# Pooled maps and row tails of a hybrid encoder step, set later behind their projections, and the first half's maps moved to another pair of PSUM banks

## The chip, the cores and the metric

The kernel runs on one core of one Trainium2 chip. The metric is the device time of one execution in microseconds (us), as the median of several runs. A core has five engines that work at the same time, each through its own list of instructions and strictly in the order of that list: TensorE (PE in the profile; PEld is its weight load), VectorE (DVE), ScalarE (ACT), GpSimd (POOL) and SyncE (SP), whose list holds DMA issues. An instruction that waits for another engine's result holds up everything behind it in its own list.

## The reference, cut to what matters

One layer over a prompt of 2048 frames and 64 frames of a second stream. The part that the change touches is the B-branch: `u`, one of the blocks of the input projection, is averaged over a trailing window, mapped by a small matrix per group, scaled and gated.

```python
z = h @ w_in                                  # q, k, v, ga, u, gb, mg, side by side
...
for g, w in enumerate(POOL_WINDOWS):          # 2, 4, 8, 16; 256 channels each
    outs.append((hi - lo) / cnt - uf[..., sl])            # trailing mean minus self
p = jnp.einsum('btgc,gcd->btgd', p.reshape(b, t, 4, 256), w_pool)      # the map
pb = p.reshape(b, t, POOL_WIDTH) * pool_scale
...
y_b = (pb * jax.nn.silu(gb)) @ w_br_b         # the gate rows: silu(gb)
...
pp_l.append(u[:, -POOL_BUF:])                 # last 15 rows of u go out: the tails
```

## The kernel before

All matrices are float32. A product is done in three matmuls, with each operand split into a high and a low part (`hi` and `lo`; the casts and subtractions of line 82 and 83 make the parts).

The rows are worked in two halves: half 0 holds 1024 prompt frames and the 64 frames of the second stream, half 1 the other 1024 prompt frames. Channels stand on the partitions, frames along the free dimension. `proj` does one slab of 128 output channels: per row group (512, 256 and 320 frames wide in half 0; twice 512 in half 1) it runs 24 matmuls into one PSUM tile named `pj` (lines 319 to 321), then calls an evacuation, and it hands control back after every six matmuls, so also in the middle of a row group. PSUM is given out in pools of two tiles for each of the names `pj`, `z`, `tr` and `att`, eight banks in all.

`pool_group` does one window group: two slabs of `u`. Their evacuation (`evac_u`) copies the rows to SBUF (line 395), saves the last 15 columns in `hist` (line 396) and, for the 64 frames, in `shist` (line 403), sums over the window on DVE (lines 368 and 377, in `pooled`), and splits the result into `phi` and `plo`, of which three buffers each exist. Behind the second slab come two maps (`mapped`), one for each 128 output channels: six matmuls (lines 423 to 425) into one PSUM tile, then one DVE instruction that scales by `pscale` and multiplies by the gate row `gbl` (line 427), and a store. `tail_out` turns the 15 saved rows on PE (line 437), copies them on ACT (line 439) and stores them.

Beside half 0's later projections runs the attention of the 64 frames (`sample_stream`): key chunks turned into `tr` tiles (line 761), scores into two `z` tiles (lines 780 and 781), which ACT copies (line 785) and DVE adds up (line 786), then sigmoids, a scan (line 622) and products (line 830). Half 1's pooled groups stand alone between projections.

What order stands on PE is set by a planner in the kernel. It keeps a clock of estimated matmul time in ns; `run` takes from several generators in turn; `defer(delay, fn)` puts a piece of work aside until that clock has gone on by the delay, and `settle`, called after every step of `run`, does what is due. PE's list is then kept as written. The lists of DVE, ACT, POOL and SP are ordered, in these stages, by the framework's scheduler from the same program.

Of the kernel before, what the change touches and what calls it, by code (L numbers as in the profile page):

```python
# [8 lines left out]
F32 = mybir.dt.float32  # L9
# [6 lines left out]
P = 128  # L16
# [7 lines left out]
RA = SEQ // 2 + DEC  # L24
# [20 lines left out]
def kernel(  # L45
# [6 lines left out]
    nc = tc.nc  # L52
# [12 lines left out]
    gb_d = dram.tile([D, R], F32, name="gb_d")  # L65
# [11 lines left out]
    def split(hi, lo, src, eng=None):  # L77

        if eng == "v":
            nc.vector.tensor_copy(hi, src)  # L80
        else:
            nc.scalar.copy(hi, src)  # L82
        (nc.gpsimd if eng == "g" else nc.vector).tensor_tensor(lo, src, hi.bitcast(F32), op=ALU.subtract)  # L83
# [23 lines left out]
    def mm_ns(n):  # L107
        return max(107.0, n * 0.4167)

    def defer(delay, fn):  # L110
        waiting.append((clock[0] + delay, fn))
# [37 lines left out]
    with ExitStack() as front:  # L149
        pool = front.enter_context(tc.tile_pool(name="front", bufs=1, side="left"))  # L150
        psum = front.enter_context(tc.tile_pool(name="fpsum", bufs=2, space=PSUM))
# [3 lines left out]
        attp = attx.enter_context(tc.tile_pool(name="attp", bufs=1, side="right"))  # L155

        def stage(name):
            return side.tile([P, 528], F32, name=name, tag="st", bufs=4)
# [9 lines left out]
        hist = side.tile([P, KT, BUF], F32, name="hist")  # L168
        shist = side.tile([P, KT, BUF], F32, name="shist")
# [24 lines left out]
        def gain_row():  # L194
            ones = side.tile([P, P], F32, name="ones", tag="sgs", bufs=2)
            nc.gpsimd.memset(ones[0:1], 1.0)
            row = attp.tile([P, 2, 512], F32, name="g_row", tag="v", bufs=4)
            nc.sync.dma_start(row[0:1], norm_g[0:1].rearrange("o (b c) -> o b c", b=2))
            return ones, row
# [127 lines left out]
        def groups_of(half):  # L327
            return GROUPS_A if half == 0 else GROUPS_B
# [22 lines left out]
        def pool_group(half, gi):  # L351
            w = WINDOWS[gi]
            groups = groups_of(half)
            parts, gates = {}, {}

            wraw = pool.tile([P, 2, 256], F32, name="wraw", tag="raw", bufs=3)
            nc.sync.dma_start(wraw, w_pool[0, gi].rearrange("(k p) c -> p k c", p=P))
            wphi = side.tile([P, 2, 256], F32R, name="wphi")
            wplo = side.tile([P, 2, 256], F32R, name="wplo")
            split(wphi, wplo, wraw)  # L360

            def pooled(hi, lo, t0, n, ext, start):

                cur, width = ext, 1
                while width < w:
                    nxt = side.tile([P, 528], F32, name=f"s{2 * width}")
                    c0 = BUF - w + 2 * width
                    nc.vector.tensor_tensor(nxt[:, c0:BUF + n], cur[:, c0:BUF + n],
                                            cur[:, c0 - width:BUF + n - width], op=ALU.add)
                    cur, width = nxt, width * 2  # L370
                b0 = w if start else 0
                if start:
                    nc.vector.tensor_tensor(cur[:, BUF:BUF + w], cur[:, BUF:BUF + w], icnt[:, 0:w], op=ALU.mult)
                    nc.vector.tensor_tensor(cur[:, BUF:BUF + w], cur[:, BUF:BUF + w], ext[:, BUF:BUF + w],
                                            op=ALU.subtract)
                res = cur[:, BUF + b0:BUF + n]
                nc.vector.scalar_tensor_tensor(res, res, 1.0 / w, ext[:, BUF + b0:BUF + n],
                                               op0=ALU.mult, op1=ALU.subtract)
                split(hi[:, t0:t0 + n], lo[:, t0:t0 + n], cur[:, BUF:BUF + n])

            def evac_u(s):
                c = gi * 2 + s

                def evac(g, c0, n, ps):
                    hi = side.tile([P, 512], F32R, name="phi", tag="qhi", bufs=3)
                    lo = side.tile([P, 512], F32R, name="plo", tag="qlo", bufs=3)
                    parts[s, g] = (hi, lo)
                    ext = stage("ext")
                    last = g == len(groups) - 1
                    npr = min(n, 1024 - c0)  # L390
                    if g == 0 and half == 0:
                        nc.gpsimd.memset(ext[:, 0:BUF], 0.0)
                    else:
                        nc.vector.tensor_copy(ext[:, 0:BUF], hist[:, c, :])
                    nc.scalar.copy(ext[:, BUF:BUF + npr], ps[:, 0:npr])
                    nc.vector.tensor_copy(hist[:, c, :], ext[:, npr:npr + BUF])
                    if half == 1 and last:
                        defer(2500, lambda: tail_out(c, hist[:, c, :], pool_prompt))
                    if npr < n:
                        es = stage("es")  # L400
                        nc.vector.tensor_copy(es[:, 0:BUF], shist[:, c, :])
                        nc.scalar.copy(es[:, BUF:BUF + DEC], ps[:, npr:n])
                        nc.vector.tensor_copy(shist[:, c, :], es[:, DEC:DEC + BUF])
                        defer(2500, lambda: tail_out(c, shist[:, c, :], pool_sample))
                        pooled(hi, lo, npr, DEC, es, False)
                    pooled(hi, lo, 0, npr, ext, half == 0 and g == 0)
                    if s == 1:
                        for t in range(2):
                            row, r0 = (gi * 2 + t) * P, half * RA + c0
                            gates[t, g] = attp.tile([P, 528], F32, name="gbl", tag="be", bufs=8)  # L410
                            nc.sync.dma_start(gates[t, g][:, 0:n], gb_d[row:row + P, r0:r0 + n])
                        defer(8000, lambda: mapped(g, c0, n, 0))
                        defer(8000, lambda: mapped(g, c0, n, 1))
                return evac

            def mapped(g, c0, n, s):
                r0 = half * RA + c0
                c = gi * 2 + s
                pb = psum.tile([P, 512], F32, name="z")
                co = slice(s * P, (s + 1) * P)  # L420
                for k in range(2):
                    hi, lo = parts[k, g]
                    nc.tensor.matmul(pb[:, 0:n], wphi[:, k, co], hi[:, 0:n], start=k == 0, stop=False)
                    nc.tensor.matmul(pb[:, 0:n], wphi[:, k, co], lo[:, 0:n], start=False, stop=False)
                    nc.tensor.matmul(pb[:, 0:n], wplo[:, k, co], hi[:, 0:n], start=False, stop=k == 1)
                bt = gates[s, g]
                nc.vector.scalar_tensor_tensor(bt[:, 0:n], pb[:, 0:n], pscale[:, c:c + 1], bt[:, 0:n],
                                               op0=ALU.mult, op1=ALU.mult)
                nc.sync.dma_start(bT_d[c * P:(c + 1) * P, r0:r0 + n], bt[:, 0:n])
                return 6 * mm_ns(n)  # L430


            yield from proj(groups, [(OFF_U + (gi * 2 + s) * P, evac_u(s)) for s in range(2)])

        def tail_out(c, src, dst):
            tr = psum.tile([P, 512], F32, name="tr")
            nc.tensor.transpose(tr[0:BUF, 0:P], src, ident)
            t = side.tile([P, P], F32, name="tl", tag="sgs", bufs=2)
            nc.scalar.copy(t[0:BUF], tr[0:BUF, 0:P])
            nc.sync.dma_start(dst[0, 0, :, c * P:(c + 1) * P], t[0:BUF])  # L440
            return 107.0
# [443 lines left out]
        with tc.manual_schedule(engines={E.Activation, E.DVE, E.SP}):  # L885
# [10 lines left out]
            row = gain_row()  # L896
# [99 lines left out]
        for g in range(4):  # L996
            rest += [proj(GROUPS_B, [branch_gate(1, c)]) for c in (2 * g, 2 * g + 1) if c > 3]
            rest.append(pool_group(1, g))
# [122 lines left out]
    def kept(ps, name):  # L1121
        t = kept_tile(name)
        if len(ps.shape) == 2:
            t = t.rearrange("p a b -> p (a b)")[0:ps.shape[0], 0:ps.shape[1]]
        nc.scalar.copy(t, ps)
        return t
# [78 lines left out]
    with tc.manual_schedule(engines={E.PE, E.DVE, E.Activation, E.SP}):  # L1205
        gates = ctx.enter_context(tc.tile_pool(name="gates", bufs=1, side="left"))
# [107 lines left out]
        for s, (i, t, p) in enumerate(order):  # L1314
            r = rf.pop(s)
            more = s - p + 7 < len(order)
            for cc in range(2):
# [5 lines left out]
                for j in range(2):  # L1323
                    c = 2 * cc + j
# [97 lines left out]
        def accumulator(nm):  # L1422
            return bpsum.tile([P, 2, 512], F32, name=nm)[:, 0]

        for n, (_, r) in enumerate(pairs):
# [11 lines left out]
            z = accumulator("y")  # L1437
# [22 lines left out]
            if n == 0:  # L1460
# [5 lines left out]
                for b in range(2):  # L1466
                    t = gates.tile([P, 2, NR], F32, name="fg_bc", tag="sg", bufs=5)
# [31 lines left out]
        for b, terms in enumerate((((0, "b11"), (1, "b21")), ((0, "b11"), (0, "t1"), (1, "b22")))):  # L1499
# [14 lines left out]
            t = kept(ps[DEC:P], "low")  # L1514
# [36 lines left out]
```

## Time and profile before

| What | Number |
|---|---|
| Median of three runs (lowest, highest) | 2735.23 us (2733.71, 2737.06) |
| The profiled execution, its own time | 2733.61 us |
| Span in its profile, first to last instruction | 2731.9 us |
| Mean granted TensorE clock | 0.997 |
| PE, busy | 2688.7 us, 98% |
| PEld, busy | 2359.8 us, 86% |
| DVE, busy | 1833.8 us, 67% |
| ACT, busy | 1268.7 us, 46% |
| Maps: matmuls of lines 423 to 425 | 240, from 631.9 to 2063.6 us of the span |
| Tails: transposes of line 437 | 16, from 642.6 to 2054.2 us |

A busy time is the sum of an engine's instructions as the profiler has them. Matmuls overlap: the next starts before the last has left the array, so a row of PE shows a duration that is longer than the step to the next row, and a pause of PE shows as idle only as far as it is longer than that overlap. "Idle before" names what ended a pause. The half-0 maps lie between 631 and 1020 us, the half-1 maps between 1918 and 2064 us.

### The profile page before, as it was taken

The numbers are of one execution on the slowest core, as the hardware profiler recorded it, in microseconds if no ns is written. First come the engines' busy times: TensorE is split into PE (matmuls) and PEld (weight loads), VectorE is DVE, ScalarE is ACT, GpSimd is POOL, SyncE is SP. The second block draws the span as 40 slices with busy tenths as digits, with TensorE's granted clock in tenths as the row PEclk, the third lists the DMA queues.
The fourth block names the chain that finished last, engine by engine and source line by source line (L and its number), as shares of the span: only waits on it lengthen the run. The fifth ranks groups of instructions, "written<-read, shape, count | busy, mean of one in ns | idle before, by whom it ended". The sixth has DMA issues, their size and how long they took to land.

```text
span 2731.9 us, 41957 instructions
## 1 busy us (share of the span) xinstructions
PE 2688.7 (98%) x15128; PEld 2359.8 (86%) x15128; DVE 1833.8 (67%) x2872; ACT 1268.7 (46%) x2527; POOL 557.3 (20%) x1269
## 2 busy tenths in 40 slices
PE   8999999999999999999999999999999999999997
PEld 7999999988998989888888888888888889999886
DVE  6555555567777684587878888786553236777886
ACT  5446444455555553455555555564222223333443
POOL 1122222220000000122433342342004601111011
PEclk9999999999999999999999999999999999999999
DMA  4224222234444444311111111112336857786753
GB/s 142 83 86 129 73 73 73 79 108 149 152 156 144 153 147 158 90 47 54 55 47 51 53 49 43 55 47 81 101 104 217 268 188 261 264 284 227 249 161 120
DMA packets 343824, 342.84 MB, mean 125 GB/s; under 512 B 29999, under 2 KB 286495, under 8 KB 343614
## 3 DMA queue, kind: packets, MB, share of 16 engines
q1 hardware_dynamic: 329182, 293.21, 34.2%
q0 software_dynamic: 14432, 46.93, 4.8%
q8 instruction: 119, 1.95, 0.3%
q14 instruction: 91, 0.75, 0.1%
HBM read 231.41 MB, written 108.65 MB: 124 GB/s over the span
## 4 chain that ended last, share of the span: by engine, by line
PE 83%; DVE 7%; issue 6%; ACT 2%; POOL 1%; DMA 1%; POOLq 0%; SPq 0%; DVEq 0%; ACTq 0%
PE pj L319 17%; PE pj L320 17%; PE pj L321 17%; PE tr L681 4%; PE att L698 2%; PE att L697 2%; PE att L696 2%; PE z L670 2%; PE z L669 2%; PE z L668 2%; PE x L1111 2%; PE x L1113 2%; PE x L1115 2%; PE y L1111 1%; PE y L1113 1%
## 5 line engine op out<-in xcount | busy, mean ns | idle before, releaser
L319 PE MATMUL pj<-hhi,whi 128*128 128x512 f32 (+2 forms) x2568 | 928.0, 361 | 0.5 <-ACT hhi L913 0.5
L321 PE MATMUL pj<-hhi,wlo 128*128 128x512 f32 (+2 forms) x2568 | 900.5, 351 | 0.0
L320 PE MATMUL pj<-hlo,whi 128*128 128x512 f32 (+2 forms) x2568 | 899.5, 350 | 0.8 <-DVE hlo L916 0.7
L321 PEld LDWEIGHTS pj<-hhi,wlo 128*128 128x128 f32 x2568 | 484.8, 189 | 61.1
L319 PEld LDWEIGHTS pj<-hhi,whi 128*128 128x128 f32 x2568 | 486.8, 190 | 57.3 <-ACT hhi L913 1.2
L320 PEld LDWEIGHTS pj<-hlo,whi 128*128 128x128 f32 x2568 | 486.2, 189 | 55.4 <-DVE hlo L916 1.5
L622 DVE TENSOR_TENSOR_SCAN om<-om 128x513 f32<-128x513 f32 (+3 forms) x356 | 387.2, 1088 | 206.0 <-POOL om L604 106.9
L612 ACT ACTIVATE om<-z 128x512 f32<-128x512 f32 (+2 forms) x320 | 171.6, 536 | 304.7 <-PE z L670 253.7
L83 DVE TENSOR_TENSOR wlo<-raw,whi 128x512 fp32r<-128x512 f32 x248 | 177.8, 722 | 183.7 <-ACT whi L82 183.1
L624 POOL COPY carry<-om 128x1 f32<-128x1 f32 x356 | 78.6, 221 | 914.0 <-DVE om L622 871.2
L625 DVE TENSOR_TENSOR be<-be,om 128x512 f32<-128x512 f32 (+3 forms) x356 | 230.3, 647 | 32.6 <-POOL carry L624 0.5
L82 ACT CAST whi<-raw 128x512 fp32r<-128x512 f32 x251 | 155.1, 623 | 174.1 <-PE pj L320 156.3
L82 ACT CAST a<-tr 128x512 fp32r<-128x512 f32 (+2 forms) x356 | 188.1, 528 | 97.1 <-PE tr L681 86.1
L83 DVE TENSOR_TENSOR a<-tr,a 128x512 fp32r<-128x512 f32 (+2 forms) x356 | 215.2, 605 | 23.9 <-ACT a L82 21.9
L681 PE MATMUL tr<-ident,be 128*128 128x128 f32 x1088 | 176.2, 274 | 3.9 <-DVE be L625 3.7
L681 PEld LDWEIGHTS tr<-ident,be 128*128 128x128 f32 x1088 | 136.2, 140 | 41.1 <-DVE be L625 9.3
L613 ACT ACTIVATE be<-z 128x512 f32<-128x512 f32 (+2 forms) x320 | 170.0, 531 | 0.0
L696 PE MATMUL att<-a,v 128*128 128x512 f32 (+1 forms) x320 | 132.6, 414 | 0.0
L617 POOL COPY om<-carry 128x1 f32<-128x1 f32 x224 | 123.6, 552 | 2.7 <-DVE be L625 0.7
L604 POOL TENSOR_SCALAR_AFFINE_SELECT om<-om 128x128 f32<-128x128 f32 x128 | 50.6, 395 | 355.8 <-ACT om L612 355.8
L698 PE MATMUL att<-a,v 128*128 128x512 f32 (+1 forms) x320 | 118.6, 371 | 3.9 <-DVE a L83 3.5
L670 PE MATMUL z<-khi,qlo 128*128 128x512 f32 (+2 forms) x320 | 116.8, 365 | 0.0
(333 smaller groups left out, 4744.5 us busy)
## 6 DMA issues: line engine op xcount, KB each, us to landing
raw<-in_w_in_dram SPq DMA_DIRECT2D x253, 256.0 KB, 3.0
sg<-sm_d SPq DMA_DIRECT2D x48, 352.0 KB, 6.4
kraw<-in_cache_k_dram SPq DMA_DIRECT2D x64, 256.0 KB, 3.1
vraw<-in_cache_v_dram SPq DMA_DIRECT2D x64, 256.0 KB, 2.8
sm_d<-sgm SPq DMA_DIRECT2D x48, 256.0 KB, 2.4
wraw<-tw_d SPq DMA_DIRECT2D x24, 512.0 KB, 4.5
out_dram<-nat SPq DMA_DIRECT2D x42, 256.0 KB, 2.3
r<-aT_d SPq DMA_DIRECT2D x12, 704.0 KB, 7.3
```

The lines of the kernel that those rows point to most:

```text
L82: nc.scalar.copy(hi, src)
L83: (nc.gpsimd if eng == "g" else nc.vector).tensor_tensor(lo, src, hi.bitcast(F32), op=ALU.subtract)
L319: nc.tensor.matmul(ps[:, 0:n], whi[:, k], hhi[:, k, c0:c0 + n], start=k == 0, stop=False)
L320: nc.tensor.matmul(ps[:, 0:n], whi[:, k], hlo[:, k, c0:c0 + n], start=False, stop=False)
L321: nc.tensor.matmul(ps[:, 0:n], wlo[:, k], hhi[:, k, c0:c0 + n], start=False, stop=k == KT - 1)
L612: nc.scalar.activation(om[:, off:512], z[:, off:512], AF.Sigmoid, scale=-SCALE)
L622: nc.vector.tensor_tensor_scan(rev, rev, rev, 1.0, op0=ALU.mult, op1=ALU.bypass)
L625: nc.vector.tensor_tensor(be[:, off:512], be[:, off:512], om[:, off + 1:513], op=ALU.mult)
L670: nc.tensor.matmul(z[:, off:512], qlo[:, qs], khi[:, 0:m], start=False, stop=True)
L681: nc.tensor.transpose(tr[:, i * P:(i + 1) * P], be[:, off + j * P:off + (j + 1) * P], ident)
L696: nc.tensor.matmul(self.acc[:, s], vhi[:, js], ahi[:, s], start=first, stop=False)
L698: nc.tensor.matmul(self.acc[:, s], vhi[:, js], alo[:, s], start=False, stop=last)
```

## The change

Four things are altered. The tails are put aside for 9000 ns of the planner's clock and not 2500. The two maps of a row group are put aside for 10500 ns and not 8000. The gate rows are no longer fetched in the evacuation but by a function of their own (`load_gates`), put aside for 4000 ns. And in half 0 a map's PSUM tile is taken from the name `pj`, the projections' two banks, where it was one of the two `z` banks; half 1 keeps `z`.

```diff
-                        defer(2500, lambda: tail_out(c, hist[:, c, :], pool_prompt))
+                        defer(9000, lambda: tail_out(c, hist[:, c, :], pool_prompt))
...
-                        defer(2500, lambda: tail_out(c, shist[:, c, :], pool_sample))
+                        defer(9000, lambda: tail_out(c, shist[:, c, :], pool_sample))
                         pooled(hi, lo, npr, DEC, es, False)
                     pooled(hi, lo, 0, npr, ext, half == 0 and g == 0)
                     if s == 1:
+                        defer(4000, lambda: load_gates(g, c0, n))
                         for t in range(2):
-                            row, r0 = (gi * 2 + t) * P, half * RA + c0
-                            gates[t, g] = attp.tile([P, 528], F32, name="gbl", tag="be", bufs=8)
-                            nc.sync.dma_start(gates[t, g][:, 0:n], gb_d[row:row + P, r0:r0 + n])
-                        defer(8000, lambda: mapped(g, c0, n, 0))
-                        defer(8000, lambda: mapped(g, c0, n, 1))
+                            defer(10500, lambda t=t: mapped(g, c0, n, t))
                 return evac
+
+            def load_gates(g, c0, n):
+                for t in range(2):
+                    row, r0 = (gi * 2 + t) * P, half * RA + c0
+                    gates[t, g] = attp.tile([P, 528], F32, name="gbl", tag="be", bufs=8)
+                    nc.sync.dma_start(gates[t, g][:, 0:n], gb_d[row:row + P, r0:r0 + n])
 
             def mapped(g, c0, n, s):
...
-                pb = psum.tile([P, 512], F32, name="z")
+                pb = psum.tile([P, 512], F32, name="z" if half else "pj")
```

No instruction of an engine is added or removed; lines behind the change have numbers that are 3 higher.

The first place is PE's list at the first two maps of half 0 (window 2, frames 0 to 511). Before, they stand between two row groups; numbers tell tiles of one name apart, and a bracket names the engine whose counter the instruction waits for:

```order
L423 MATMUL z_7615<-phi_7399,wphi_7313 128x512 [waits DVE_49]
L424 MATMUL z_7615<-plo_7400,wphi_7313 128x512
L425 MATMUL z_7615<-phi_7399,wplo_7314 128x512
L423 MATMUL z_7615<-phi_7491,wphi_7313 128x512 [waits Activation_49]
L424 MATMUL z_7615<-plo_7492,wphi_7313 128x512 [waits DVE_49]
L425 MATMUL z_7615<-phi_7491,wplo_7314 128x512
L423 MATMUL z_7624<-phi_7399,wphi_7313 128x512 [waits PE_49]
L424 MATMUL z_7624<-plo_7400,wphi_7313 128x512
L425 MATMUL z_7624<-phi_7399,wplo_7314 128x512
L423 MATMUL z_7624<-phi_7491,wphi_7313 128x512
L424 MATMUL z_7624<-plo_7492,wphi_7313 128x512
L425 MATMUL z_7624<-phi_7491,wplo_7314 128x512
```

Now they stand behind four score matmuls and in the middle of a row group, `pj_7611`, of whose 24 matmuls 12 stand ahead and 12 behind (the last row is the first of these):

```order
L427 MATMUL pj_7660<-plo_7400,wphi_7313 128x512
L428 MATMUL pj_7660<-phi_7399,wplo_7314 128x512
L426 MATMUL pj_7660<-phi_7491,wphi_7313 128x512
L427 MATMUL pj_7660<-plo_7492,wphi_7313 128x512 [waits DVE_49]
L428 MATMUL pj_7660<-phi_7491,wplo_7314 128x512
L426 MATMUL pj_7669<-phi_7399,wphi_7313 128x512 [waits DVE_49]
L427 MATMUL pj_7669<-plo_7400,wphi_7313 128x512
L428 MATMUL pj_7669<-phi_7399,wplo_7314 128x512
L426 MATMUL pj_7669<-phi_7491,wphi_7313 128x512
L427 MATMUL pj_7669<-plo_7492,wphi_7313 128x512
L428 MATMUL pj_7669<-phi_7491,wplo_7314 128x512
L319 MATMUL pj_7611<-hhi_99,whi_7317 128x320
```

The waits for `phi` and `plo` lie further back now, and the second map's first matmul waits for DVE: `pj_7611` holds one of the two `pj` banks, so both maps are given the other. Of half 0's twelve pairs ten stand inside a row group in this way; two (window 2 and window 16, the 320-wide groups) stand at a group's end, where both banks can be had.

The second place is DVE's list around the same two maps. Before, their two instructions (line 427) stand among the window sums, ahead of the next score additions:

```order
L377 SCALAR_TENSOR_TENSOR s2_7606<-s2_7606,ext_7602 128x256 [waits DVE_49]
L427 SCALAR_TENSOR_TENSOR gbl_7504<-z_7615,pscale_90,gbl_7504 128x512 [waits DMAHW7_49,PE_49]
L401 COPY es_7784<-shist_93 128x15 [waits DVE_49]
L83 TENSOR_TENSOR plo_7601<-s2_7606,phi_7600 128x256 [waits Activation_49]
L427 SCALAR_TENSOR_TENSOR gbl_7506<-z_7624,pscale_90,gbl_7506 128x512 [waits DMAHW0_49,PE_49]
```

Now the score additions (line 789) stand ahead of the first, and the scan (line 625) and its product ahead of the second:

```order
L401 COPY es_7779<-shist_93 128x15 [waits DVE_49]
L83 TENSOR_TENSOR klo_7582<-tr_7618,khi_7581 128x512 [waits Activation_49]
L789 TENSOR_TENSOR be_7631<-z_7632,be_7631 64x512 [waits Activation_49]
L789 TENSOR_TENSOR be_7631<-z_7637,be_7631 64x512 [waits Activation_49]
L430 SCALAR_TENSOR_TENSOR gbl_7539<-pj_7660,pscale_90,gbl_7539 128x512 [waits DMAHW7_49,PE_49]
L625 SCALAR_TENSOR_TENSOR om_7642<-om_7642 128x513 [waits Activation_49,Pool_49]
L628 TENSOR_TENSOR be_7631<-be_7631,om_7642 128x512 [waits DVE_49,Activation_49]
L83 TENSOR_TENSOR plo_7601<-s2_7606,phi_7600 128x256 [waits Activation_49]
L430 SCALAR_TENSOR_TENSOR gbl_7541<-pj_7669,pscale_90,gbl_7541 128x512 [waits DMAHW0_49,PE_49]
```

The multiplication of the first map (now line 430) is what the second map's first matmul waits for, and it stands behind two additions here.

The third place is PE's list at the first tail of half 0. Before, it stands right behind the maps of the 256-wide group and waits for `shist`:

```order
L424 MATMUL z_7730<-plo_7601,wphi_7313 128x256
L425 MATMUL z_7730<-phi_7600,wplo_7314 128x256
L437 MATMUL tr_7739<-ident_69,shist_93 15x128 [waits DVE_49]
L319 MATMUL pj_7714<-hhi_99,whi_7327 128x320
L320 MATMUL pj_7714<-hlo_100,whi_7327 128x320
```

Now it stands one row group later, inside a 512-wide one (`pj_7803`) and ahead of four key transposes:

```order
L320 MATMUL pj_7803<-hlo_100,whi_7793 128x512
L321 MATMUL pj_7803<-hhi_99,wlo_7794 128x512
L440 MATMUL tr_7816<-ident_69,shist_93 15x128
L764 MATMUL tr_7829<-ident_69,kraw_7825 128x128 [waits DMAHW3_49,PE_49]
L764 MATMUL tr_7829<-ident_69,kraw_7825 128x128
```

It has no wait of its own left.

## The prediction

> **What bounds the kernel now.** I read the page's busy times and its chain first, then the stretches in which the maps stand, then PE's waits there, and last single rows around a map and a tail.
>
> ```profile
> PE 2688.7 (98%) x15128; PEld 2359.8 (86%) x15128; DVE 1833.8 (67%) x2872; ACT 1268.7 (46%) x2527; POOL 557.3 (20%) x1269
> PE 83%; DVE 7%; issue 6%; ACT 2%; POOL 1%; DMA 1%; POOLq 0%; SPq 0%; DVEq 0%; ACTq 0%
> ```
>
> PE is busy for 98% of the span and carries 83% of the chain: the kernel lasts as long as PE's list, and whatever makes PE stand still is added to the end. The same by stage, for the stretch of the half-0 maps and that of the half-1 maps (columns: length, busy time of PE, PEld, DVE, ACT, POOL with counts, clock, DMA share, GB/s):
>
> ```profile
> 615.00:1045.00 430.00, 424.97 (x2703) 385.50 (x2701) 320.18 (x640) 235.44 (x470) 23.18 (x77) 1.00 0.48 153
> 1880.00:2080.00 200.00, 199.86 (x888) 161.87 (x887) 102.85 (x177) 56.41 (x103) 10.93 (x16) 1.00 0.36 117
> ```
>
> In the second stretch PE is idle for 0.14 us in 200, so nothing can be won there. In the first it is idle for 5.0 us, and DVE is 74% busy: an instruction given to DVE often finds others ahead. PE's waits from 600 to 1130 us (total, count, longest):
>
> ```profile
> PE tr L437 <- DVE shist L403: 2.1, 3, 1.4
> PE z L423 <- DVE be L786: 1.2, 2, 0.8
> PE z L424 <- DVE plo L83: 0.6, 2, 0.4
> PE z L423 <- ACT phi L82: 0.5, 1, 0.5
> PE tr L845 <- DVE as L839: 0.4, 1, 0.4
> PE tr L437 <- DVE s L368: 0.2, 1, 0.2
> ```
>
> All but one row belong to maps (lines 423, 424) and tails (437): nine waits, 2.1 + 1.2 + 0.6 + 0.5 + 0.2 = 4.6 us. The rest of the kernel does not meet the change.
>
> **The waits that are removed.** A row's idle time is less than the pause, because the matmul before it is still leaving the array:
>
> ```profile
> 641.67 0.28 PE L424 MATMUL z<-plo,wphi 128*128 128x256 f32 x1
> 641.79 0.28 PE L425 MATMUL z<-phi,wplo 128*128 128x256 f32 x1
> 642.59 0.28 PE L437 MATMUL tr<-ident,shist 128*15 128x128 f32 x1 [0.52 <-DVE shist L403]
> ```
>
> Matmuls of this width start 0.12 us apart, so the transpose was due at 641.91 and came 0.68 us late, of which the row shows 0.52. With 0.16 us more for each, the nine pauses are 4.6 + 9 x 0.16 = 6.0 us. In the new order the tails stand a row group later and have no such wait in front, the maps find `phi` and `plo` long done, and they leave the `z` banks, for whose score additions (L786) two of the waits were. I take all 6.0 us as gone. Bounds: nothing removed beyond this in the trace; if a third of it comes back at the new places, 4.0.
>
> **The wait that is added.** Ten of half 0's twelve map pairs now stand inside a row group. The open row group holds one `pj` bank, both maps get the other, and the second map's first matmul waits until DVE has read out the first. PE stands still meanwhile: behind the waiting matmul in its list are the second map and the rest of the row group. Before, each map of a pair had a `z` bank of its own, and the reading out of the first ran beside the second map. The pieces of this wait, by width 512, 256 and 320, the map's last matmul first, then DVE's multiplication:
>
> ```profile
> 632.90 0.39 PE L424 MATMUL z<-plo,wphi 128*128 128x512 f32 x1
> 633.12 0.39 PE L425 MATMUL z<-phi,wplo 128*128 128x512 f32 x1
> 633.35 0.39 PE L423 MATMUL z<-phi,wphi 128*128 128x512 f32 x1
> 634.42 0.74 DVE L427 SCALAR_TENSOR_TENSOR gbl<-z,pscale,gbl 128x512 f32<-128x512 f32 x1
> 642.69 0.48 DVE L427 SCALAR_TENSOR_TENSOR gbl<-z,pscale,gbl 128x256 f32<-128x256 f32 x1
> 656.26 0.31 PE L425 MATMUL z<-phi,wplo 128*128 128x320 f32 x1
> 656.41 0.31 PE L423 MATMUL z<-phi,wphi 128*128 128x320 f32 x1
> 656.61 0.55 DVE L427 SCALAR_TENSOR_TENSOR gbl<-z,pscale,gbl 128x320 f32<-128x320 f32 x1 [0.51 <-PE z L425]
> ```
>
> The last shows an idle DVE: the matmul ends at 656.57, DVE starts at 656.61, 0.04 us later. The way back is in a wait of before:
>
> ```profile
> 882.71 0.68 DVE L786 TENSOR_TENSOR be<-z,be 64x512 f32<-64x512 f32 x1
> 883.44 0.38 PE L423 MATMUL z<-phi,wphi 128*128 128x256 f32 x1 [0.85 <-DVE be L786]
> ```
>
> DVE ends at 883.39, PE starts at 883.44: 0.05 us. So with an idle DVE a pair costs: length of the last matmul + 0.04 + multiplication + 0.05 - the step at which the next matmul would have started anyway. For 512: 0.39 + 0.04 + 0.74 + 0.05 - 0.23 = 0.99 us. For 256: 0.28 + 0.04 + 0.48 + 0.05 - 0.12 = 0.73. For 320: 0.31 + 0.04 + 0.55 + 0.05 - 0.15 = 0.80. The ten pairs are four, four and two of these: 3.96 + 2.92 + 1.60 = 8.5 us, the lower end.
>
> The upper end is DVE as late as it was before. From the start of the second map to the end of the first's multiplication it was 635.16 - 633.35 = 1.81 us in the first of the ten pairs; the widest and the last are these:
>
> ```profile
> 752.90 0.39 PE L423 MATMUL z<-phi,wphi 128*128 128x512 f32 x1
> 755.75 1.41 DVE L427 SCALAR_TENSOR_TENSOR gbl<-z,pscale,gbl 128x512 f32<-128x512 f32 x2
> 1001.23 0.28 PE L423 MATMUL z<-phi,wphi 128*128 128x256 f32 x1
> 1002.27 0.48 DVE L427 SCALAR_TENSOR_TENSOR gbl<-z,pscale,gbl 128x256 f32<-128x256 f32 x1
> ```
>
> These give about 3.56 us (the two multiplications of 1.41 us together are half each) and 1.52. All ten summed in this way are 17.2 us; with 0.05 us back each, 17.7.
>
> Between the ends I use the new order of DVE's list. Four pairs have both score additions of a chunk right ahead of the first multiplication (512 of windows 2 and 16, 256 and 320 of window 8). What these do is here:
>
> ```profile
> 637.61 0.39 PE L781 MATMUL z<-klo,q2h 128*128 128x512 f32 x1
> 638.19 1.41 DVE L786 TENSOR_TENSOR be<-z,be 64x512 f32<-64x512 f32 x2 [0.65 <-ACT be L785]
> ```
>
> The additions end at 639.60, which is 1.99 us after the last score matmul starts and 1.76 after a map behind it can start. The first map takes 6 x 0.23 = 1.37 us at 512 and 6 x 0.15 = 0.88 at 320, so DVE comes free 0.2 to 0.9 us later than PE would need it: about 2 us over the four pairs. The other six find sums and splits of 0.4 to 0.7 us ahead; at 74% busy I give them 0.4 us each, 2.4. In all 8.5 + 2.0 + 2.4 = 12.9, near the middle of the two ends (13.1); I take 13.0 us.
>
> **What is moved at no cost.** The gate rows are fetched later, in SP's list behind loads of the key and value cache:
>
> ```profile
> L411 SPq DMA_DIRECT2D gbl<-gb_d x40: 319/422/1372, 621.6 to 2033.5; - x40
> DMA to landing us min/median/max: 2.4/3.0/5.5
> ```
>
> They land 5.5 us after issue at the worst, and the planner leaves 10500 - 4000 = 6500 ns between fetch and map. That cover is 1 us thin: a row that comes late holds DVE, and now PE with it, microsecond for microsecond. The stores of the results and the turned tails wait on SP and ACT as before, only later. Maps that come later also keep `phi` and `plo` longer, of which there are three: ACT's cast for the next slab waits for the pair. ACT is 55% busy in the first stretch and 28% in the second, and PE needs ACT's evacuation of a bank only a row group of 24 matmuls later (5.5 us at 0.23), so I count nothing; without that cover each cast would hold ACT for up to the length of a pair, 2.7 us.
>
> **The clock.** After the longest of the nine waits PE's steps are what they always are, while at the kernel's start they are slower for some time:
>
> ```profile
> 13.37 0.58 PE L319 MATMUL pj<-hhi,whi 128*128 128x256 f32 x1
> 16.39 0.41 PE L321 MATMUL pj<-hhi,wlo 128*128 128x256 f32 x1
> 16.60 0.34 PE L319 MATMUL pj<-hhi,whi 128*128 128x256 f32 x1
> 16.78 0.28 PE L320 MATMUL pj<-hlo,whi 128*128 128x256 f32 x1
> 1003.49 0.28 PE L437 MATMUL tr<-ident,shist 128*15 128x128 f32 x1 [1.39 <-DVE shist L403]
> 1004.20 0.31 PE L320 MATMUL pj<-hlo,whi 128*128 128x320 f32 x1
> 1004.35 0.31 PE L321 MATMUL pj<-hhi,wlo 128*128 128x320 f32 x1
> ```
>
> At 16.4 us the step is 0.21 us for 256 columns, from 16.78 on 0.12. After a 1.39 us wait the step is 0.15 for 320, no change, and the granted clock of that stretch is 1.00, so I add nothing for the clock. [...]
>
> **The sum.** +13.0 - 6.0 = +7.0 us. Against the profiled execution's own 2733.61 us that is 2740.6. This execution lies 1.6 us under the median of the three runs, so I forecast the median at 2735.23 + 7.0 = 2742.2 us, slower by 0.26%. What a measurement can tell from no change is about 0.2%, 5.5 us.
>
> **The rivals.**
> - DVE is prompt. PE stands while it waits, DVE catches up, and pairs cost little more than 8.5 us: 8.5 - 6.0 = +2.5, 2737.7 us, no difference to be told. For it speaks that a pause gives DVE time; against it the four pairs with score additions ahead.
> - DVE is as late as before: 17.7 - 6.0 = +11.7, 2746.9 us. For it speaks the 74%; it is also where things end if a third of the removed waits comes back (+9.0, 2744.2).
> - Not slower at all. PE's rows hide a pause of up to 0.16 us under the drain; half 0 and half 1 have 20 pairs and 16 tails, 36 places with such a switch, and if each lost 0.16 us more than the idle time shows, another 5.8 us go: 8.5 - 11.8 = -3.3, 2731.9 us. The point from which it decides: a pair must cost less than a tenth of what is removed; with 6.0 us that is 0.6 us, and the shortest evacuation above needs 0.73. So it needs both the hidden pauses and a prompt DVE.
> - The clock falls after the pauses. The thirteen steps from 13.37 to 16.78 took 3.41 us and would take 13 x 0.12 = 1.56: 1.85 us lost. Ten of these: +7.0 + 18.5, 2760.7 us.
>
> **How the numbers follow.** Forecast 0.47, own range 2740.7 to 2745; prompt DVE 0.28; late DVE or returned waits 0.15; hidden pauses 0.08, half of it past the 0.2%; clock 0.02. Slower by over 0.2%: 0.47 + 0.15 + 0.02 = 0.64; within it 0.28 + 0.04 = 0.32; faster 0.04. The range goes from 2735.5 (the prompt case with some hidden pauses) to 2748.5 (the late case on the median, with a microsecond for late gate rows); outside lie most of the hidden-pause rival, the clock and the far end of the late one, about 0.15.
>
> **What the changed profile would show.** If I am right, PE's waits in the first stretch have a new row, `pj L426 <- DVE gbl L430`, ten times for about 13 us with the drain added, and the rows of lines 437, 423 and 424 (now 440, 426, 427) are gone; the second stretch stays as it is. Wrong: that row is missing or under 7 us; the old rows stand at new places; L430 waits for a DMA; or the steps behind a pause are longer than 0.23, 0.15 and 0.12 us.

## The result, and the profile after

| | Before | After |
|---|---|---|
| Median, us (lowest, highest; four runs of each on one chip) | 2735.91 (2733.71, 2737.06) | 2751.45 (2751.15, 2752.05) |
| Ratio of the times, 95% interval | | 1.0055 [1.0043, 1.0066] |
| The profiled execution, us; its span | 2733.61; 2731.9 | 2752.05; 2750.4 |
| Mean granted TensorE clock in the profile | 0.997 | 0.995 |

The change makes the kernel 0.55% slower, 15.5 us (by the interval 11.8 to 18.1), where 7.0 us were forecast. A repetition on another chip gave 2751.29 us and a ratio of 1.0051 [1.0038, 1.0065].

Busy times and chain of the page after:

```profile
PE 2694.5 (98%) x15128; PEld 2365.3 (86%) x15128; DVE 1835.3 (67%) x2872; ACT 1267.4 (46%) x2527; POOL 558.1 (20%) x1269
PE 82%; DVE 7%; issue 6%; DMA 2%; ACT 1%; POOL 1%; SPq 0%; POOLq 0%; DVEq 0%; ACTq 0%
```

PE is still the bound. The stretch of the half-1 maps, in the columns used before:

```profile
1880.00:2100.00 220.00, 219.59 (x989) 179.52 (x988) 119.31 (x199) 67.16 (x125) 19.15 (x32) 1.00 0.36 116
```

PE is idle for 0.41 us of 220 there: nothing has changed in half 1. PE's waits from 600 to 1130 us after the change:

```profile
PE pj L426 <- DVE gbl L430: 13.5, 10, 3.0
PE pj L319 <- DVE gbl L430: 2.5, 3, 0.9
PE tr L848 <- DVE as L842: 0.4, 1, 0.4
PE tr L764 <- ACT tl L442: 0.3, 1, 0.3
```

Of the six rows of before, the five of maps and tails are gone. In their place stands the forecast row, ten times, and a second one that was not forecast: three row groups (L319) that wait for the multiplication of a map.

The widest of the ten pauses, first on PE (some rows left out), then the list of DVE in that time:

```profile
1005.39 0.39 PE L428 MATMUL pj<-phi,wplo 128*128 128x512 f32 x1
1008.83 0.50 PE L426 MATMUL pj<-phi,wphi 128*128 128x512 f32 x1 [3.05 <-DVE gbl L430]
1009.40 0.43 PE L428 MATMUL pj<-phi,wplo 128*128 128x512 f32 x1
1009.63 0.62 PE L426 MATMUL pj<-phi,wphi 128*128 128x512 f32 x1
1010.05 0.63 PE L427 MATMUL pj<-plo,wphi 128*128 128x512 f32 x1
1010.91 0.47 PE L319 MATMUL pj<-hhi,whi 128*128 128x320 f32 x1
1011.17 0.47 PE L320 MATMUL pj<-hlo,whi 128*128 128x320 f32 x1
1012.77 0.44 PE L320 MATMUL pj<-hlo,whi 128*128 128x320 f32 x1
1013.04 0.32 PE L321 MATMUL pj<-hhi,wlo 128*128 128x320 f32 x1
1013.20 0.31 PE L319 MATMUL pj<-hhi,whi 128*128 128x320 f32 x1
```

```profile
1005.46 0.67 DVE L789 TENSOR_TENSOR be<-z,be 64x512 f32<-64x512 f32 x1
1006.06 0.41 DVE L83 TENSOR_TENSOR plo<-s,phi 128x256 fp32r<-128x256 f32 x1
1006.39 0.42 DVE L368 TENSOR_TENSOR s<-s 128x264 f32<-128x264 f32 x1
1006.84 0.69 DVE L789 TENSOR_TENSOR be<-z,be 64x512 f32<-64x512 f32 x1
1007.57 0.42 DVE L368 TENSOR_TENSOR s<-s 128x256 f32<-128x256 f32 x1
1008.02 0.75 DVE L430 SCALAR_TENSOR_TENSOR gbl<-pj,pscale,gbl 128x512 f32<-128x512 f32 x1
```

The first map is complete at 1005.78. DVE has five instructions ahead of its multiplication, two score additions (L789), two window sums (L368) and a split (L83), and comes to it at 1008.02; PE goes on at 1008.83, which is 3.21 us later than its step of 0.23 would have it. Then there is something else to be seen in the PE rows: from 1009.63 on, matmuls of 512 columns start 0.42 us apart and those of 320 columns 0.26 to 0.27, and from 1013.04 on 0.15 again. The granted clock from 1009.63 to 1013.04 us is 0.50, behind it, up to 1017 us, 1.00. These are eleven matmuls, three of 512 and eight of 320, which take 3.41 us and would take 3 x 0.23 + 8 x 0.15 = 1.89: 1.5 us lost.

One of the three row groups that wait:

```profile
892.75 0.31 PE L321 MATMUL pj<-hhi,wlo 128*128 128x320 f32 x1
893.98 0.50 PE L319 MATMUL pj<-hhi,whi 128*128 128x512 f32 x1 [0.92 <-DVE gbl L430]
```

The row group of 320 that was open during the pair ends, and the next one asks for the bank of the second map, which DVE (busy with a scan, a split and a product) has not read out: 1.23 - 0.15 = 1.08 us.

### The profile page after: what moved, and what is told of

The parts are those of the page before. It is cut to its first block, busy times and chain, and to the rows that moved or that the text cites. A ratio compares the mean times of both kernels' runs of the same rounds, so it can differ in the third digit from the quotient of the medians.

```text
span 2750.4 us, 41971 instructions
## 1 busy us (share of the span) xinstructions
PE 2694.5 (98%) x15128; PEld 2365.3 (86%) x15128; DVE 1835.3 (67%) x2872; ACT 1267.4 (46%) x2527; POOL 558.1 (20%) x1269
## 4 chain that ended last, share of the span: by engine, by line
PE 82%; DVE 7%; issue 6%; DMA 2%; ACT 1%; POOL 1%; SPq 0%; POOLq 0%; DVEq 0%; ACTq 0%
PE pj L319 17%; PE pj L320 16%; PE pj L321 16%; PE tr L684 4%; PE att L701 2%; PE z L673 2%; PE att L700 2%; PE att L699 2%; PE z L672 2%; PE z L671 2%; PE x L1114 2%; PE x L1118 2%; PE x L1116 2%; PE y L1114 1%; PE y L1118 1%
## 5 line engine op out<-in xcount | busy, mean ns | idle before, releaser
L319 PE MATMUL pj<-hhi,whi 128*128 128x512 f32 (+2 forms) x2568 | 929.5, 362 | 4.1 <-DVE gbl L430 2.5
L319 PEld LDWEIGHTS pj<-hhi,whi 128*128 128x128 f32 x2568 | 487.2, 190 | 63.2 <-DVE gbl L430 3.2
L83 DVE TENSOR_TENSOR wlo<-raw,whi 128x512 fp32r<-128x512 f32 x248 | 177.7, 721 | 182.3 <-ACT whi L82 181.4
L83 DVE TENSOR_TENSOR a<-tr,a 128x512 fp32r<-128x512 f32 (+2 forms) x356 | 215.3, 605 | 26.5 <-ACT a L82 24.5
```

The source lines that it names most:

```text
L319: nc.tensor.matmul(ps[:, 0:n], whi[:, k], hhi[:, k, c0:c0 + n], start=k == 0, stop=False)
```

## The experiments

Theory A: the added time is PE standing at ten pairs that share one bank, plus the row groups behind them; the length of each is the read-out and what its engine has ahead of it. Theory B: the longer distances themselves cost, by late gate rows or by `phi` and `plo` held longer. Theory C: behind some long pauses of PE the clock falls for one stretch, as behind the pause above (3.05 us idle, then 3.41 us at a granted clock of 0.50, 1.5 us lost), and behind one of up to 1.39 us, the longest idle time of before in half 0, it does not; which pauses in between have such a stretch is open.

**The distances without the banks.**

```diff
-                pb = psum.tile([P, 512], F32, name="z" if half else "pj")
+                pb = psum.tile([P, 512], F32, name="z")
```

> The changed kernel with the z banks in both halves, so that only the three distances (tails, maps, gate rows) differ from before. Theory A (the added time is PE standing at the ten map pairs that share one pj bank, 15.1 us, with 2.9 us of row groups that wait for the second map's bank behind it): all of that goes, the removed tail waits stay removed, 2730 to 2735 us; the row of pj L426 waiting for L430 is gone, a few waits of z L426 for score additions (L789) of up to 3 us in all may stand in its place. Theory B (the longer distances themselves cost, by late gate rows or by phi and plo held longer): 2745 us or more, the bank making little difference.

Measured: 2736.55 us, ratio to before 0.9998 [0.9989, 1.0006]. The wait of L426 for L430 is gone; from 600 to 1130 us there is now

```profile
PE z L426 <- DVE be L789: 4.2, 4, 1.8
```

B falls: the distances add nothing. The time is 1.6 us above the range given for A, since the waits for score additions, 1.2 us before, are 4.2 here: in three of the four places the maps now stand right behind score matmuls that fill both `z` banks.

**The banks without the distances.**

```diff
-                pb = psum.tile([P, 512], F32, name="z")
+                pb = psum.tile([P, 512], F32, name="z" if half else "pj")
```

> The kernel before with nothing but the bank changed: half 0's maps in pj, at the old distances. By its order eight of the twelve pairs (four 256 wide, three 320, one 512) then stand inside a row group. Theory A: eight pauses of 1.0 to 1.7 us, 8 to 13 us, less some 1.5 us of waits for z banks that go: 2742 to 2748 us, with a row of pj L423 waiting for L427 eight times. Theory B (the distances cost): within 2 us of before, 2734 to 2738 us.

Measured: 2758.12 us, ratio 1.0082 [1.0068, 1.0095], above what A gave. Its largest waits from 600 to 1130 us:

```profile
PE pj L423 <- DVE gbl L427: 11.2, 8, 2.5
PE pj L319 <- DVE gbl L427: 3.7, 4, 2.1
PE pj L423 <- ACT es L402: 1.7, 2, 1.1
```

The eight pauses are there, 11.2 us, but so are four row groups behind a pair (3.7) and two first maps that come before ACT has emptied a row group's bank (1.7). The trace also has three stretches of half clock in half 0, behind the pauses at 645, 883 and 1020 us, 1.5 us each (mean granted clock of this profile 0.994, of before 0.997). The bank is enough to make the kernel slow; with the longer distances, in the changed kernel, it costs less.

**Six matmuls or more between the maps of a pair.**

```diff
-                            defer(10500, lambda t=t: mapped(g, c0, n, t))
+                            defer(10500 + 3000 * t, lambda t=t: mapped(g, c0, n, t))
```

> The changed kernel, but the second map of a pair is put aside 3000 ns longer than the first, so that six or more projection matmuls stand between them and DVE can read out the first map meanwhile; banks, tails and gate rows as changed. Theory A: 10 of the pauses at the second map shrink from 15.1 us to under 3 us; row groups that begin behind a second map may wait for it, 2 to 4 us; 2730 to 2737 us. Theory B: unchanged, 2748 to 2753 us.

Measured: 2735.0 us, ratio 0.9995 [0.9986, 1.0004], with the same banks as the changed kernel:

```profile
PE pj L426 <- DVE gbl L430: 1.5, 2, 1.3
PE pj L319 <- DVE gbl L430: 0.8, 1, 0.8
PE pj L319 <- ACT sgm L337: 0.5, 1, 0.5
```

The 13.5 us of the ten pauses become 1.5: it is the two maps back to back in one bank that cost, not the bank as such.

**The pairs only between row groups.** A flag, set while a row group is open, holds half 0's maps back until it has ended.

```diff
+                        is_open[0] = k < KT - 1
...
-            due = [w for w in waiting if final or w[0] <= clock[0]]
+            due = [w for w in waiting if final or w[0] <= clock[0] - 1e9 * (is_open[0] and len(w) > 2)]
...
-                            defer(10500, lambda t=t: mapped(g, c0, n, t))
+                            defer(10500, lambda t=t: mapped(g, c0, n, t), *[1] * (half == 0))
```

> The changed kernel, but half 0's maps are done only where no row group is open, so that both pj banks can be had; the second map then waits for ACT's copy out of the row group that has just ended, which runs beside the first map. Theory A: no wait of the second map for L430; the first matmul of the next row group waits for the first map's multiplication instead, which runs beside the second map, so a few tenths each: 2731 to 2740 us. Theory B: 2748 to 2753 us, as the distances are the same.

Measured: 2741.05 us, ratio 1.0012 [1.0003, 1.0021], 1 us above A's range.

```profile
PE pj L322 <- DVE gbl L433: 4.1, 5, 2.3
PE pj L429 <- ACT es L405: 2.9, 3, 1.8
```

No second map waits for the first, but the row group behind a pair does (5 times), and the second map waits for ACT (3 times): "a few tenths each" was too low, since one took 2.3 and one 1.8 us of idle time.

**One map in each kind of bank.**

```diff
-                pb = psum.tile([P, 512], F32, name="z" if half else "pj")
+                pb = psum.tile([P, 512], F32, name="z" if half or s else "pj")
```

> The changed kernel, but only the first map of a pair in half 0 goes to pj and the second to z, so that neither waits for the other; the z bank it asks for had the whole first map's time (0.7 to 1.4 us) to come free from the score additions. Theory A: none of the ten waits for L430 at the second map, no row group that waits behind it (the first map's bank is read out while the second runs), under 1.5 us of waits for L789; of the 6 us of waits in the kernel before some 4 to 5 stay removed: 2731 to 2735 us beside 2737 of before, the fastest of all so far. If instead the tails' and gate rows' new places cost something by themselves: 2737 or more.

Measured: 2730.53 us, ratio to before 0.9976 [0.9968, 0.9985], the fastest of all, faster than before and after, and 0.5 us under A's range. All of PE's waits from 600 to 1130 us:

```profile
PE tr L764 <- DVE klo L83: 0.8, 1, 0.8
PE z L426 <- DVE be L789: 0.4, 1, 0.4
PE tr L848 <- DVE as L842: 0.4, 1, 0.4
PE tr L440 <- DVE klo L83: 0.2, 1, 0.2
```

With the ten pauses away, 6.6 us of the time before are gone (by the interval 4.1 to 8.8). Three of these waits (L764, L426 and L440) are 1.8 us from start to start less the step, so of the 6.0 us that the prediction removes some 4 should be left here; the interval holds both numbers, and the removal is real. With both maps in `z` at the same distances it did not show, because waits for score additions took its place.

**DVE taken out of the wait.** ACT copies half 0's maps out of their bank, and DVE multiplies from the copy.

```diff
+                if half:
+                    nc.vector.scalar_tensor_tensor(bt[:, 0:n], pb[:, 0:n], pscale[:, c:c + 1], bt[:, 0:n],
...
+                else:
+                    mo = outgoing("mo")
+                    nc.scalar.copy(mo[:, 0:n], pb[:, 0:n])
+                    nc.vector.scalar_tensor_tensor(bt[:, 0:n], mo[:, 0:n], pscale[:, c:c + 1], bt[:, 0:n],
...
```

> The changed kernel, but in half 0 ACT copies a map's tile out of its bank and DVE multiplies from the copy in SBUF; banks and distances as changed. It takes DVE's list out of the wait. Theory A: the pauses remain, as both maps still share a bank, but each is the copy (0.58 us at 512, 0.35 at 256) and what ACT, 55% busy, has ahead of it: 0.8 to 1.3 us a pair, 8 to 12 us instead of 15.1, and none over 2 us; 2741 to 2748 us. If the long pauses came from the bank's release itself and not from DVE's list: about 2751 as the changed kernel.

Measured: 2739.32 us, ratio 1.0008 [0.9999, 1.0016], under A's range.

```profile
PE pj L426 <- ACT mo L435: 6.2, 10, 1.0
PE pj L319 <- ACT mo L435: 0.2, 1, 0.2
```

The same ten places wait, 6.2 us in place of 13.5 and none over 1.0; the row groups behind them almost not at all. Of these 7.3 us some 1.4 are the shorter read-out (in this trace 0.58, 0.37 and 0.42 us at 512, 256 and 320 columns, against 0.75, 0.48 and 0.55 on DVE: 4 x 0.17 + 4 x 0.11 + 2 x 0.13); the other 5.9 are put down to what DVE had ahead of it. ACT was prompter than I took it to be.

**Half 1 as a quiet place to measure a pair.** Half 0 in `z`, half 1 in `pj` with its maps at 9000, so that all eight pairs stand inside a row group.

```diff
-                            defer(10500, lambda t=t: mapped(g, c0, n, t))
+                            defer(9000 if half else 10500, lambda t=t: mapped(g, c0, n, t))
...
-                pb = psum.tile([P, 512], F32, name="z" if half else "pj")
+                pb = psum.tile([P, 512], F32, name="pj" if half else "z")
```

> The changed kernel with the banks exchanged: half 0's maps in z, half 1's in pj and put aside for 9000 and not 10500, so that all eight pairs of half 1 stand inside a row group, 512 wide, where DVE is about half busy. It is the quiet control for the next kernel. Theory A (a pair in one bank costs the read-out and what DVE has ahead of it): eight pauses of 0.99 us (DVE idle) to 1.4 us in half 1, 8 to 11 us over the kernel with z in both halves (2736.6), so 2744 to 2748. [...] Without A: 2736 to 2738.

Measured: 2746.71 us, ratio 1.0031 [1.0019, 1.0044]. Behind 1130 us the trace has the row

```profile
PE pj L426 <- DVE gbl L430: 7.1, 8, 1.2
```

Seven of the eight start 1.23 or 1.24 us after the matmul before, 1.00 us late, and one 1.33 late: 8.3 us. The prediction's lower end for 512 columns, 0.99 us with DVE idle, is right to 0.01 us. No slow stretch follows any of them: the granted clock from 1900 to 2110 us is 1.00.

**The same pairs, read out three times as long.** Each map tile of half 1 is multiplied by 1.0 in place, twice, ahead of its multiplication.

```diff
+                for _ in range(2 * half):
+                    nc.vector.tensor_scalar(out=pb[:, 0:n], in0=pb[:, 0:n], scalar1=1.0, scalar2=None, op0=ALU.mult)
```

> The same with two more passes of DVE over each of half 1's map tiles ahead of its multiplication (times 1.0, in place), so that each of the eight pauses grows by two passes of some 0.7 us, to about 2.4 us from start to start (2.25 idle). Theory A alone: plus 8 x 1.4 to 1.5 = 11 to 12 us over the control. [...]

Measured: 2769.77 us, ratio to before 1.0118 [1.0104, 1.0131], 23.1 us over its control. Two waits of this kernel behind 1130 us, and a piece of one of its slow stretches, 3.6 us long (clock: third number from the end):

```profile
PE pj L426 <- DVE gbl L432: 19.4, 8, 2.8
PE pj L319 <- ACT ext L395: 3.8, 4, 1.0
```

```profile
1928.60:1932.20 3.60, 3.60 (x10) 2.35 (x8) 2.15 (x3) 0.31 (x1) 0.00 (x0) 0.56 0.19 71
```

The pauses grow by 19.4 - 7.1 = 12.3 us, and row groups that wait for ACT, which had not been expected, add 3.8 us of idle time. Behind four of the eight pauses, at 1929, 1946, 2021 and 2079 us, stands a stretch of half clock: 4 x 1.5 = 6.0 (the granted clock from 1900 to 2110 us is 0.97, in the control 1.00). Together 22.1 of the 23.1 us. The control, with pauses of 1.23 us at the same places, has none there; its profile has one at 2259 us that this one has not, so the account is good to some 2 us.

**Second profiles, of after and of before.**

> The changed kernel once more, for a second profile. Theory A: the same ten pauses at the second map within 0.2 us each, 15 us together, and three row groups behind them, 2.9 us: they are set by the order of DVE's list. [...]

After again: 2751.29 us, and the waits from 600 to 1130 us read to the tenth as in the first profile. A holds: they are set by the order of the lists. Of slow stretches there are three in both profiles, behind the same pauses (the granted clock from 1000 to 1025 us is 0.93 in both); I had expected them at other places, which did not come true: against the pauses the stretches lay only 0.7 us earlier. Of before:

> The kernel before once more, for a second profile. Theory C: its pauses in half 0 (up to 1.39 us) bring no slow stretch in any execution, so there is none between 600 and 1130 us; one may stand behind the wait of two steps near 1153 us (0.62 and 1.61 us idle), and its time then lies about 1.5 us above that of the first profile, 2735 us.

Before again: 2737.05 us. Its waits in half 0 are those of the first profile, and there is no slow stretch there; but near 1155 and 2575 us there is one each, where the first profile had none. The stretch from 1150 to 1175 us, in the first profile of before and in this one:

```profile
1150.00:1175.00 25.00, 22.77 (x117) 18.43 (x116) 21.03 (x29) 14.16 (x30) 7.41 (x24) 1.00 0.08 24
```

```profile
1150.00:1175.00 25.00, 22.77 (x108) 18.34 (x107) 19.78 (x26) 12.97 (x27) 6.37 (x20) 0.93 0.06 18
```

The clock is 1.00 and 0.93 there, and from 2570 to 2595 us 1.00 and 0.93 as well. So two of the three slow stretches of the changed kernel (at 1170 and 2590 us) belong to waits that the kernel before has too, and that bring one in some executions and not in others; the one at 1009 us belongs to the change. With two of them this execution took 3.4 us more than the first. Of the thirteen profiles of this case twelve, all but the first of before, have a stretch of half clock that begins between 1150 and 1180 us, and four have one that begins between 2570 and 2595 us. The two second profiles, each with both, are 2751.73 - 2737.05 = 14.7 us apart.

**The tails alone.**

```diff
-                        defer(2500, lambda: tail_out(c, hist[:, c, :], pool_prompt))
+                        defer(9000, lambda: tail_out(c, hist[:, c, :], pool_prompt))
...
-                        defer(2500, lambda: tail_out(c, shist[:, c, :], pool_sample))
+                        defer(9000, lambda: tail_out(c, shist[:, c, :], pool_sample))
```

> The kernel before with the tails alone put aside for 9000 and not 2500; maps, gate rows and banks as before. Theory A: the waits of transposes L437 for shist and s go, 2.3 us of idle time and 4 x 0.16 under the drain, 2.9 us; the maps' 2.3 us (waits for z banks, phi and plo) stay: 2.9 us under before, 2733 to 2735 beside 2737. If the tails' later place costs (a tr bank that a key chunk needs, as L764 waiting for L442), 2736 or more.

Measured: 2734.93 us, ratio 0.9988 [0.9979, 0.9997], 3.3 us less by the ratio and within the range. Its map waits are 3.0 us where before had 2.3, and one transpose of a key chunk waits for a tail's copy (0.3).

## Why the prediction was wrong in size

The direction, the place and the count of the added wait were right; the sum was about half of what came. By its own steps:

- **The waits that are removed, -6.0: right.** The rows of lines 437, 423 and 424 are gone, and the kernel with one map in each kind of bank, which has none of the pauses, is 6.6 us faster than before. One small wait came back (L764 for the tail's copy), 0.62 us from start to start, 0.5 over the step of 0.11.
- **The wait that is added, +13.0: 2.1 us short.** From start to start, less the step, the ten pauses are 1.20, 1.03, 1.00, 0.95, 0.81, 2.51, 1.73, 1.51, 3.21 and 1.17: 15.1 us. The lower ends hold (0.99 predicted, 1.00 measured in half 1). "Four pairs about 2 us over" is what failed: over their lower ends these four are 0.21, 2.22, 1.00 and 0.71, 4.1 in all. I had counted the additions up to their end; in DVE's list the second stands behind sums, and another sum stands behind it, so the multiplication of the 3.21 us pause began 2.24 us after its operands were complete. The other six, put at 2.4, came to 2.5, but that is luck: "0.4 us each" was wrong for them, since five have 0.01 to 0.44 over their lower ends and the sixth (512 wide, window 8) has 1.52.
- **A term that is missing: the row groups behind a pair, 2.9 us** (0.82, 1.08, 1.03). The prediction asked who waits for the first map's bank inside a pair, and not who wants either bank next. Both banks of `pj` are in use at that moment, so the next row group must wait for one of them: twice for the second map's, once, at 661 us behind a pair that stands between two row groups, for the first map's. Each time DVE's multiplication stands behind a scan and a product.
- **The clock, "I add nothing": 1.5 us.** The inference from nine pauses of up to 1.39 us was right for such pauses (the eight of half 1, up to 1.2 us idle, have no slow stretch either) and was carried to pauses that were forecast only as a mean of 1.3 but reached 3.2. The rival of a falling clock has a slow stretch behind each of the ten, 1.85 us each; the profiles show one behind one of ten, 1.5 us, so neither reading was right.
- **What is moved at no cost: right.** L430 waits for no DMA in the trace after, and the distances alone change nothing that can be measured. One thing speaks against "the rest of the kernel does not meet the change": in both traces after, a row group at 2185 us waits for ACT (L319 for L337, 1.2 and 0.7 us idle, 1.4 and 0.9 from start to start less the step), and in neither trace of before. Why is open.

The sum with the measured terms: 15.1 + 2.9 + 1.5 + 0.5 - 6.0 = +14.0 us, without the wait at 2185 us. That is within the interval of the result (11.8 to 18.1) and beside the 12.6 us of the second chip and the 14.7 us between the two second profiles. The 18.5 us between the spans of the two first profiles have 3.0 us more for the two stretches of half clock that before did not happen to have in that execution. The forecast's range went up to 2748.5; the late rival, 2746.9 by DVE as late as before, had the pauses at 17.7 and nothing behind them, and also missed.

What is not settled: single runs of before spread over 10 us (2732.43 to 2742.90 in 27 runs); how much of that the stretches of half clock make, which only profiled executions show, was not measured.

## What to carry to other kernels

If two accumulations are put back to back into a pool of two banks while a third is open, price three things: the read-out of the first (here 0.8 us at 320 columns and 1.0 at 512 for an idle engine), everything that stands ahead of it in its engine's list up to the instruction itself, and the next owner of the second bank. With the two results in different pools the cost was gone and the benefit of the move stayed (2730.5 us); with a few matmuls between them the cost was gone, but a benefit could not be told (2735.0 us, ratio to before 0.9995). And look at the longest pause that a change can make, not at the mean: here single pauses of up to 1.4 us cost their own length (1.39 us idle in before, 1.2 in half 1), and of the longer ones some cost another 1.5: one of 3.05 us idle did, one of 2.36 did not, and one of 1.78 did in one kernel and not in another.

## What was not expected of the hardware

In the trace after, stretches of half clock begin at 1009.63, 1170.06 and 2590.02 us (a matmul in which the step changes is divided by its length). Each lasts 3.4 us: the granted clock is 0.50 from 1009.63 to 1013.04, from 1170.06 to 1173.47 and from 2590.02 to 2593.43 us, and behind them the steps are again 0.15 us at 320 columns (the first) and 0.23 at 512 (the two others). The pauses ahead of them left PE idle for 3.05, 1.94 and 2.09 us.

A shorter one was followed by such a stretch too: 1.78 us, ahead of half 0's first map of pooling window 16, in the kernel with half 1 in `pj`:

```profile
993.25 0.40 PE L784 MATMUL z<-klo,q2h 128*128 128x512 f32 x1
995.43 0.50 PE L426 MATMUL z<-phi,wphi 128*128 128x512 f32 x1 [1.78 <-DVE be L789]
995.76 0.59 PE L427 MATMUL z<-plo,wphi 128*128 128x512 f32 x1
996.14 0.63 PE L428 MATMUL z<-phi,wplo 128*128 128x512 f32 x1
996.57 0.63 PE L426 MATMUL z<-phi,wphi 128*128 128x512 f32 x1
```

From 996.14 us on the steps are 0.43 us. The kernel with the distances alone has the same pause of 1.78 us at the same place, and behind it its steps stay at 0.23. Nor does such a stretch follow the pause of 2.36 us in the trace after, from 878.7 to 881.0 us: the granted clock from 877 to 886 us is 1.00.

Two shorter ones close together stood ahead of another stretch, in the kernel with half 1 in `pj` again. The 3.41 us ahead of it, and the stretch (clock: third number from the end):

```profile
2255.32:2258.73 3.41, 1.93 (x10) 1.40 (x10) 2.39 (x2) 2.25 (x2) 0.00 (x0) 1.00 1.05 379
2258.73:2262.14 3.41, 3.41 (x14) 3.41 (x13) 3.34 (x5) 0.00 (x0) 0.35 (x1) 0.50 0.72 222
```

Two pauses of 0.25 and 1.23 us lie in the first of these lines; the clock of the second is 0.50. The first profile of before has two pauses of 0.62 and 1.61 us between 1152 and 1155 us, and its clock stays at 1.00; its second profile has a stretch of half clock near 1155 us. So in these traces the length of a pause alone does not tell whether a slow stretch follows, and the same program can have one in one execution and not in another. What else decides is not shown here.
